# Side work kept in traced order, two more deferred key projections, later marks, a longer lead, and pair scans that carry their own first column

## The chip, the cores and the metric

The kernel runs on one core of one Trainium2 chip. The metric is the device time of one execution in microseconds (us), median over runs; lower is better.

## The reference

Two layers over a prompt of 2048 frames and a sample group of 64 frames (1024 features, 16 heads of 64). Layer 0 ("A") is attention in a band of chunks with a softmax; layer 1 ("B") is stick-breaking attention over all earlier frames, with a running product instead of a softmax. Both have a gate, an output projection and a residual.

```python
# layer 0, mixer A: per query chunk of 64, own chunk and 8 before it
q, k, v, gate = split(rms_norm(x, g) @ w_in_a)
x = x + (softmax(q @ k.T * SCALE + rel_bias, masked) @ v * silu(gate)) @ w_out_a
# shared keys and values, then layer 1, mixer B
k, v = split(rms_norm(x, g_kv) @ w_kv);  q, gate = split(rms_norm(x, g_b) @ w_in_b)
z = q @ k.T * SCALE;  log_fail = where(mask, log_sigmoid(-z), 0)
later = reverse_cumsum(log_fail) - log_fail
x = x + ((where(mask, exp(log_sigmoid(z) + later), 0) @ v) * silu(gate)) @ w_out_b
y = rms_norm(x)
```

Outputs are y for both groups and the new key and value rows of both layers.

## The kernel before

Every projection product is made from two parts of each operand (a rounded high part and the rest), so each block of 128 x 512 results takes 24 matmuls: 8 slices of the 1024 features, three products each. TensorE does these, the scores, the 128 x 128 turns ("flip") of attention weights, and the products with the values.

There are four stages in time. **A's projections** (`projections("a", ...)`): norms, values, then for each kind (k, q, gate) and each of the 8 head pairs `hp` two halves of 1024 frames. Where `(kind, hp)` is in `DEFER`, the second half is left out there and done later as side work. **A's attention** runs from about 753 us to 1335 us: head pair by head pair, 512-query groups in the order `ORDER = [(1, 0), (3, 2)]`. Then the rest of A's output projection; then **B's projections** and, from about 2078 us to 3260 us, **B's attention** in the same order (both with sample items beside), and the rest of B's output projection.

In an attention stage the class `Beat` writes the order of the code. One beat is one query tile: its scores, the turn and split of an older tile (`LAG`), the products of one older still (`HOLD`). `RATE` (0.4 a beat in A, 0.3 in B) lets in steps of side work from the list `beside`: late jobs (`late_job`: the deferred halves; 8 steps of 6 matmuls each, tile `ps_j`), the loading and splitting of the output weights (`w_out_steps`, tiles `woraw` to `big`), and output tiles (`out_tile`, tile `ps_o`, 8 steps of 6 matmuls each). Each unit of side work has `load` (DMAs issued on SP), `cut` (ACT rounds to the high part, DVE takes the rest) and the product steps. `load` of the next unit goes beside the first step of the present one, its `cut`s beside the second half. `lead(LEAD)` does the first steps before the first attention item. `when_summed` puts a group's output tiles on the list once its last head pair is done; they read back (`og`) what the attention stored (`o_a`, `o_b`).

The code's order is not the order of the engines' queues. A planner in the framework reorders the instructions of each engine's queue by its own cost estimates, under the data dependencies. `InOrder` can pin an instruction behind the one traced before it on its engine (`keep_in_program_order`), but its switch `order.on` is False everywhere in this kernel, so nothing is pinned.

In B, `pass_sticks` takes the running product over 512 keys, from the last to the first, two at a time: ACT makes `f`, POOL multiplies neighbours into `two` (256 columns), DVE scans `two` into every second column of `s`, and `between` on POOL first copies the carry (one column) into `s` and then fills the columns in between. Diagonal blocks scan all columns directly.

```python
            def between():
                to, carry = st
                gps.tensor_copy(to[:, CH : CH + 1], carry)
                gps.tensor_tensor(to[:, 1:CH:2], by2[:, :, 1], to[:, 2 : CH + 1 : 2], ALU.mult)
```

## Time and profile before

| what | value |
|---|---|
| time, median of 3 runs | 3362.42 us (3362.26 to 3369.03) |
| profiled execution, its own time | 3363.2 us |
| its span, first to last instruction | 3361.4 us |
| TensorE busy share, matmul / weight load | 96% / 83% |
| DVE, ACT, POOL busy share | 56%, 51%, 38% |

How to read it: PE is TensorE's matmuls, PEld its weight loads, DVE the vector engine, ACT the scalar engine, POOL GpSimd, SP the engine that issues most DMAs; a trailing q (SPq) is an engine's sequencer issuing or waiting. Each engine works its queue in order, so an instruction that waits holds all behind it. Almost all compute shows line L86, the helper that records every operation, so groups are told apart by the tiles that they write and read.

### The profile page before, as it was taken

What the parts mean: (1) busy time and instruction counts of PE and PEld (TensorE: products, weight loads), DVE (VectorE), ACT (ScalarE), POOL (GpSimd) and SP (SyncE); (2) the same over time, 40 slices, a digit from 0 to 9 for tenths busy, and PEclk for the clock granted to TensorE, in tenths of its full rate; (3) what the DMA queues carried; (4) which work ended last, traced back from release to release, by engine and by line L of the source; (5) the groups of instructions that cost most, each with busy time, mean ns of one, the idle gap of its engine ahead of it and who ended that gap; (6) DMA issues with size and microseconds to landing.
All of it is one profiled execution on the core that took longest, in us unless ns stands there. A gap on an engine that the chain in (4) does not pass through costs nothing.

```text
span 3361.4 us, 53483 instructions
## 1 busy us (share of the span) xinstructions
PE 3232.5 (96%) x17928; PEld 2801.8 (83%) x17928; DVE 1896.1 (56%) x3815; ACT 1723.1 (51%) x3716; POOL 1282.4 (38%) x1929
## 2 busy tenths in 40 slices
PE   8999999998999999999999999999999999999998
PEld 6889999986888888878889998778788787888777
DVE  3224431116886776322033333888888889888773
ACT  4323322226996776233144433666666676666661
POOL 2002210004774454021044200444476767777760
PEclk9999999998999999999999999999999999999999
DMA  5459984248998875544399857666735564445523
GB/s 188 140 176 362 338 318 155 95 146 258 253 241 221 240 215 151 188 138 137 106 338 352 294 184 226 178 186 189 192 103 140 155 181 127 129 128 152 139 89 110
DMA packets 454409, 643.30 MB, mean 191 GB/s; under 512 B 49733, under 2 KB 269925, under 8 KB 454134
## 3 DMA queue, kind: packets, MB, share of 16 engines
q1 hardware_dynamic: 394678, 588.75, 57.0%
q10 hardware_dynamic: 59456, 51.13, 4.7%
q8 instruction: 143, 2.34, 0.3%
q14 instruction: 132, 1.08, 0.1%
HBM read 388.85 MB, written 250.90 MB: 190 GB/s over the span
## 4 chain that ended last, share of the span: by engine, by line
PE 60%; DVE 7%; ACT 4%; DMA 3%; issue 3%; POOL 1%; SPq 0%; ACTq 0%; POOLq 0%; DVEq 0%
PE ps_o L86 10%; PE acc L86 10%; PE ps_t L86 10%; PE z L86 9%; PE wt L86 8%; PE ps_v L86 6%; PE ps_j L86 5%; DVE s L86 3%; DVE pl L86 2%; ACT ph L86 1%; ACT s L86 1%; DMA o_a<-ot 1%; ACT f L86 0%; DVE ol L86 0%; PE ps_tr L86 0%
## 5 line engine op out<-in xcount | busy, mean ns | idle before, releaser
L86 DVE TENSOR_TENSOR pl<-wt,ph 128x512 fp32r<-128x512 f32 (+1 forms) x864 | 551.8, 654 | 135.8 <-ACT ph L86 132.3
L86 ACT ACTIVATE ph<-wt 128x512 fp32r<-128x512 f32 (+1 forms) x864 | 483.7, 577 | 200.3 <-PE wt L86 183.4
L86 PE MATMUL wt<-ident,s 128*128 128x128 f32 x3472 | 552.6, 276 | 21.0 <-DVE pl L86 11.7
L86 PE MATMUL ps_t<-x_own,wh 128*128 128x362 f32 (+1 forms) x2304 | 569.9, 328 | 0.0
L86 PEld LDWEIGHTS wt<-ident,s 128*128 128x128 f32 x3472 | 418.5, 141 | 94.0 <-DVE pl L86 14.4
L86 ACT ACTIVATE f<-z 128x512 f32<-128x512 f32 (+4 forms) x680 | 355.3, 535 | 223.4 <-PE z L86 132.7
L86 POOL TENSOR_TENSOR s<-f,s 128x256 f32<-128x256 f32 x416 | 363.4, 874 | 122.0 <-DVE s L86 108.7
L86 PEld LDWEIGHTS ps_t<-x_own,wh 128*128 128x128 f32 x2304 | 404.8, 188 | 1.9
L86 PE MATMUL acc<-ph,vt 128*128 128x512 f32 (+3 forms) x1088 | 376.8, 381 | 20.5 <-ACT ph L86 14.3
L86 PE MATMUL acc<-pl,vt 128*128 128x512 f32 (+3 forms) x1088 | 368.3, 372 | 27.2 <-DVE pl L86 25.4
L86 PE MATMUL z<-kt,q 128*128 128x512 f32 (+3 forms) x1280 | 376.2, 381 | 11.3 <-ACT f L86 10.1
L86 PE MATMUL ps_t<-x_own,wl 128*128 128x362 f32 (+1 forms) x1152 | 377.4, 328 | 0.0
L86 POOL TENSOR_SCALAR s<-s,rc 128x640 f32<-128x640 f32 (+5 forms) x264 | 195.5, 748 | 469.6 <-DVE rc L86 419.0
L86 PE MATMUL ps_o<-big,oh 128*128 128x512 f32 x1088 | 338.8, 394 | 0.3 <-DVE pl L86 0.3
L86 POOL TENSOR_TENSOR two<-f 128x256 f32<-128x256 f32 x416 | 265.7, 641 | 168.4 <-ACT f L86 158.2
L86 DVE TENSOR_TENSOR_SCAN s<-two,s,own 128x256 f32<-128x256 f32 x408 | 299.6, 738 | 47.6 <-POOL two L86 41.9
L86 PE MATMUL ps_t<-big,wh 128*128 128x512 f32 x960 | 298.3, 391 | 0.0
L86 PEld LDWEIGHTS z<-kt,q 128*128 128x128 f32 x1280 | 220.3, 191 | 47.0 <-ACT f L86 23.8
L86 PEld LDWEIGHTS acc<-pl,vt 128*128 128x128 f32 x1088 | 196.2, 191 | 69.3 <-DVE pl L86 53.7
L86 PEld LDWEIGHTS acc<-ph,vt 128*128 128x128 f32 x1088 | 200.1, 192 | 46.6 <-ACT ph L86 21.0
L86 PEld LDWEIGHTS ps_o<-big,oh 128*128 128x128 f32 x1088 | 203.3, 189 | 42.0 <-DVE pl L86 0.9
L86 PEld LDWEIGHTS ps_t<-x_own,wl 128*128 128x128 f32 x1152 | 216.3, 188 | 0.1
(142 smaller groups left out, 5487.1 us busy)
## 6 DMA issues: line engine op xcount, KB each, us to landing
vt<-v_b SPq DMA_DIRECT2D x80, 512.0 KB, 5.1
v_b<-vs SPq DMA_DIRECT2D x64, 512.0 KB, 5.5
q<-q_a SPq DMA_DIRECT2D x128, 256.0 KB, 6.2
q<-q_b SPq DMA_DIRECT2D x128, 256.0 KB, 4.2
vt<-v_a SPq DMA_DIRECT2D x48, 512.0 KB, 8.1
kt<-k_b SPq DMA_DIRECT2D x96, 256.0 KB, 5.7
keys<-k_a SPq DMA_DIRECT2D x80, 256.0 KB, 6.7
v_a<-vs ACTq DMA_DIRECT2D x32, 512.0 KB, 2.7
```

The lines of the kernel that those rows point to most:

```text
L86: ins = op(*args, **kwargs)
```

## The change

1. `DEFER["a"]` holds the second half of the keys of head pairs 4 to 7 instead of 6 and 7: two more late jobs in A's attention.
2. `in_place` pins the `load` and `cut` steps of all side work to the traced order of SP, ACT and DVE while `order.amid` is set, that is from the end of `lead` to the end of the items. Products and what stands behind them are not pinned.
3. `SETTLE = 5`: output tiles come on the list five beats later.
4. `LEAD["b"]` is 14 instead of 8.
5. In the projections the sample's doubled columns live in a tile `x_new` of the pool tag `ol`, filled by two POOL copies, where `x_own[0]` had 64 more columns, filled by one ACT copy; the norm's `junk` gets a buffer of its own.
6. `two` becomes three persistent tiles of 257 columns whose last column is one. The scan runs over 257 columns and writes the carry itself (carry times one); the POOL copy in `between` goes.

```diff
--- before.py
+++ after.py
@@ -39,15 +39,17 @@
 
 SAMPLE = {(1, 0): [4, 3], (3, 2): [2, 1, 0]}
 
-DEFER = dict(a=[("k", 6), ("k", 7)], b=[(k, hp) for k in "gq" for hp in range(HP)])
+DEFER = dict(a=[("k", hp) for hp in (4, 5, 6, 7)], b=[(k, hp) for k in "gq" for hp in range(HP)])
 
 RATE = dict(a=0.4, b=0.3)
 LAG = dict(a=2, b=5)
 
-LEAD = dict(a=8, b=8)
+LEAD = dict(a=8, b=14)
 HOLD = dict(a=1, b=2)
 
 STEP = 2
+
+SETTLE = 5
 TOK = [(t * P, min(P, T - t * P)) for t in range((T + P - 1) // P)]
 
 HALF = NP // 2
@@ -73,7 +75,8 @@
 
 
     def __init__(self, tc):
-        self.tc, self.on = tc, False
+
+        self.tc, self.on, self.amid = tc, False, False
 
     def engine(self, engine):
         outer = self
@@ -99,6 +102,18 @@
     order = InOrder(tc)
     dve, act, gps, pe = (order.engine(x) for x in (nc.vector, nc.scalar, nc.gpsimd, nc.tensor))
     mm = pe.matmul
+
+    def in_place(what):
+
+
+        def pinned():
+            was, order.on = order.on, order.amid
+            what()
+            order.on = was
+
+        return pinned
+
+    sp = order.engine(nc.sync)
 
     cpool = ctx.enter_context(tc.tile_pool(name="consts", bufs=1))
     dram = ctx.enter_context(tc.tile_pool(name="scratch", bufs=1, space=DRAM))
@@ -194,17 +209,18 @@
             tc.tile_pool(name=f"pp_{L}", bufs=1, space=PSUM) as psum,
         ):
 
-
-            x_own = [xpool.tile([P, NK, HALF + m], F32R, name=f"x_own{i}") for i, m in enumerate((2 * NS, NS))]
+            x_own = [xpool.tile([P, NK, HALF + NS], F32R, name=f"x_own{i}") for i in range(2)]
             x_big = big_pair()
             xs = [x_own, x_big]
             with tc.tile_pool(name=f"v_{L}", bufs=2) as pool:
+
+                x_new = []
 
                 def normed(t, scale=gps.tensor_scalar):
                     r0, n = TOK[t]
                     xt = pool.tile([P, D], F32, name="xt", tag="xt", bufs=3)
                     nc.sync.dma_start(xt[:n], x_of(t))
-                    junk = opool.tile([P, D], mybir.dt.bfloat16, name="junk", tag="xr", bufs=2)
+                    junk = pool.tile([P, D], mybir.dt.bfloat16, name="junk", tag="junk", bufs=1)
                     r = rstd_of(pool, xt, n, junk)
                     scale(xt[:n], xt[:n], r[:n], 1.0, ALU.mult, ALU.mult)
                     ps = psum.tile([P, NK, P], F32, name="ps_tr", tag="tr", bufs=1)
@@ -213,7 +229,10 @@
                     hf, c = spot(r0)
                     split(*(x[:, :, c : c + n] for x in xs[hf]), ps[:, :, :n])
                     if n == NS:
-                        act.activation(x_own[0][:, :, NEW + NS :], f32(x_own[1][:, :, NEW:]), AF.Copy)
+
+                        x_new.append(opool.tile([P, NK, P], F32R, name="x_new", tag="ol", bufs=2))
+                        for i in range(2):
+                            gps.tensor_copy(x_new[0][:, :, i * NS : i * NS + NS], f32(x_own[i][:, :, NEW:]))
 
                 seq = [t for gs_ in ORDER for g in gs_ for t in range(4 * g, 4 * g + 4)] + [len(TOK) - 1]
                 if L == "a":
@@ -244,7 +263,7 @@
                         out = ps[:n]
                         if n == NS:
                             for k in range(NK):
-                                both = x_own[0][:, k, NEW:]
+                                both = x_new[0][:, k]
                                 mm(ps, both, wh[k], start=(k == 0), stop=False)
                                 mm(ps, both, wl[k], start=False, stop=(k == NK - 1))
                             out = pool.tile([P, CH], F32, name="vn", tag="vn", bufs=2)[:n]
@@ -638,7 +657,7 @@
         def load():
             st["raw"] = opool.tile([P, NK, P], F32, name="lraw", tag="og", bufs=1)
             c = c0 + hp * P
-            nc.sync.dma_start(st["raw"], w[:, c : c + P].rearrange("(k p) c -> p k c", p=P))
+            sp.dma_start(st["raw"], w[:, c : c + P].rearrange("(k p) c -> p k c", p=P))
             st["wh"] = opool.tile([P, NK, P], F32R, name="lwh", tag="oh", bufs=2)
             st["wl"] = opool.tile([P, NK, P], F32R, name="lwl", tag="ol", bufs=2)
 
@@ -694,7 +713,7 @@
             rows = kind == "k" and HALF + c >= first
             behind.append([partial(out, c)] + ([partial(add_back, c), (2, partial(token_rows, c))] if rows else []))
         products = [partial(some, c, k0) for c in chunks for k0 in range(0, NK, STEP)]
-        return [load] + [partial(cut, k0) for k0 in range(0, NK, STEP)], products, behind
+        return [in_place(x) for x in [load] + [partial(cut, k0) for k0 in range(0, NK, STEP)]], products, behind
 
     def w_out_steps(src, w):
 
@@ -704,7 +723,7 @@
             if k < NK:
                 tag = ("oh", "ol")[k % 2]
                 raws[k] = opool.tile([P, D], F32, name="woraw", tag=tag, bufs=2)
-                nc.sync.dma_start(raws[k], src[k * P : (k + 1) * P])
+                sp.dma_start(raws[k], src[k * P : (k + 1) * P])
 
         def cut(k):
             if k == 0:
@@ -715,7 +734,11 @@
             del raws[k]
 
         return [
-            ([partial(load, i) for i in range(3)] if k == 0 else [], [None], [[partial(cut, k), partial(load, k + 3)]])
+            (
+                [in_place(partial(load, i)) for i in range(3)] if k == 0 else [],
+                [None],
+                [[in_place(partial(cut, k)), in_place(partial(load, k + 3))]],
+            )
             for k in range(NK)
         ]
 
@@ -733,9 +756,9 @@
         def load():
             st["og"] = opool.tile([P, NK, P], F32, name="og", tag="og", bufs=1)
             src = lay[L]["o"][g][:, :, c0 : c0 + n].rearrange("k p t -> p k t")
-            nc.sync.dma_start(st["og"][:, :, :n], src)
+            sp.dma_start(st["og"][:, :, :n], src)
             st["xr"] = opool.tile([P, D], F32, name="xr", tag="xr", bufs=2)
-            nc.sync.dma_start(st["xr"][:n], residual(t))
+            sp.dma_start(st["xr"][:n], residual(t))
             st["oh"] = opool.tile([P, NK, P], F32R, name="oh", tag="oh", bufs=2)
             st["ol"] = opool.tile([P, NK, P], F32R, name="ol", tag="ol", bufs=2)
 
@@ -776,7 +799,7 @@
 
         products = [partial(some, c, k0) for c in range(0, D, CH) for k0 in range(0, NK, STEP)]
         cuts = [partial(cut, k0) for k0 in range(0, NK, NK // 2)]
-        return [load] + cuts, products, [[partial(out, 0)], [partial(out, CH), finish]]
+        return [in_place(x) for x in [load] + cuts], products, [[partial(out, 0)], [partial(out, CH), finish]]
 
     class Beat:
 
@@ -851,6 +874,7 @@
                 n -= 1
                 self.ready = 0
                 self.step()
+            order.amid = True
 
         def products(self):
             while self.held and self.held[0][0] + self.hold <= self.clock:
@@ -903,11 +927,12 @@
 
         def when_summed(self, what):
 
-            self.marks.append((self.blocks[-1][0] + 2 + self.hold, what))
+            self.marks.append((self.blocks[-1][0] + 2 + self.hold + SETTLE, what))
 
         def end(self):
             while self.tiles or self.blocks or self.held or self.marks:
                 self.beat()
+            order.amid = False
             while self.now or self.beside:
                 self.ready = 0
                 self.step()
@@ -1211,27 +1236,32 @@
                 return [lambda: None, scan]
 
             by2 = f.rearrange("p (j i) -> p j i", i=2)
-            two = pool.tile([P, CH // 2], F32, name="two", tag="two", bufs=2)
+            two = twos[0]
+            twos.append(twos.pop(0))
 
             def pairs():
-                gps.tensor_tensor(two, by2[:, :, 0], by2[:, :, 1], ALU.mult)
+                gps.tensor_tensor(two[:, :-1], by2[:, :, 0], by2[:, :, 1], ALU.mult)
 
             def scan():
                 to, carry = pr(), carry_in()
-                st.extend((to, carry))
+                st.append(to)
+
                 dve.tensor_tensor_scan(
-                    to[:, CH - 2 :: -2], two[:, ::-1], own[:, : CH // 2], carry, ALU.mult, ALU.bypass
+                    to[:, ::-2], two[:, ::-1], own[:, : CH // 2 + 1], carry, ALU.mult, ALU.bypass
                 )
                 passed(to[:, x0 : x0 + 1])
 
             def between():
-                to, carry = st
-                gps.tensor_copy(to[:, CH : CH + 1], carry)
+                to = st[0]
                 gps.tensor_tensor(to[:, 1:CH:2], by2[:, :, 1], to[:, 2 : CH + 1 : 2], ALU.mult)
 
             st = []
             return [pairs, scan, between]
 
+
+        twos = [wpool.tile([P, CH // 2 + 1], F32, name=f"two{i}") for i in range(3)]
+        for two in twos:
+            gps.memset(two[:, CH // 2 :], 1.0)
 
         totals = [wpool.tile([P, 2 * NS], F32, name=f"total{i}") for i in range(HP)]
         carries = [wpool.tile([P, 1], F32, name=f"carry{i}") for i in range(HP)]
```

## Rows read from the trace of the kernel before

**Rows 1.** The page, part 1: busy us (share of the span) xinstructions.

```profile
PE 3232.5 (96%) x17928; PEld 2801.8 (83%) x17928; DVE 1896.1 (56%) x3815; ACT 1723.1 (51%) x3716; POOL 1282.4 (38%) x1929
```

**Rows 2.** Windows: length, busy us of PE, PEld, DVE, ACT, POOL, clock, DMA.

```profile
220.00:753.00 533.00, 531.58 (x2867) 487.77 (x2866) 162.59 (x405) 155.42 (x392) 54.37 (x49) 1.00 0.68 237
753.00:860.00 107.00, 88.44 (x501) 76.49 (x502) 69.65 (x196) 73.69 (x172) 49.75 (x57) 0.92 0.89 263
860.00:1005.00 145.00, 134.13 (x913) 120.87 (x911) 120.41 (x371) 137.26 (x326) 106.16 (x129) 0.99 0.92 245
1005.00:1060.00 55.00, 48.52 (x295) 43.13 (x295) 36.07 (x90) 37.51 (x80) 23.84 (x26) 0.94 0.77 210
2080.00:2130.00 50.00, 41.92 (x212) 33.61 (x211) 34.22 (x57) 26.78 (x64) 16.46 (x29) 0.90 0.80 220
2760.00:2800.00 40.00, 31.42 (x151) 22.83 (x150) 38.91 (x56) 29.73 (x58) 25.38 (x38) 0.91 0.60 192
2800.00:3260.00 460.00, 448.05 (x2521) 367.02 (x2521) 388.47 (x613) 297.96 (x584) 338.11 (x614) 1.00 0.45 127
```

**Rows 3.** Timeline of TensorE, 755 to 770 us: start, duration, instruction.

```profile
759.63 0.62 PE L86 MATMUL ps_j<-big,lwh 128*128 128x512 f32 x2
...
762.80 0.39 PE L86 MATMUL ps_j<-big,lwl 128*128 128x512 f32 x1
```

**Rows 4.** Tile lraw: engine, operation, count, ns min/median/max.

```profile
L86 DVE SCALAR_TENSOR_TENSOR lwl<-lraw,g_b,lwh x128: 321/344/1369, 2054.5 to 2672.1; 128x128 fp32r<-128x128 f32 x128
L86 ACT ACTIVATE lwh<-lraw,g_a x16: 385/390/402, 727.9 to 754.1; 128x128 fp32r<-128x128 f32 x16
L86 DVE SCALAR_TENSOR_TENSOR lwl<-lraw,g_a,lwh x16: 350/352/353, 728.3 to 754.5; 128x128 fp32r<-128x128 f32 x16
```

**Rows 5.** Instructions on tile ps_j.

```profile
L86 ACT ACTIVATE sp<-ps_j x20: 575/597/605, 759.2 to 2760.5; 128x512 fp32r<-128x512 f32 x20
L86 DVE TENSOR_TENSOR sp<-ps_j,sp x20: 666/691/693, 759.8 to 2761.1; 128x512 fp32r<-128x512 f32 x20
```

**Rows 6.** Timeline, 1008 to 1015 us: start, duration, instruction, [idle before, releaser].

```profile
1008.10 0.37 SPq L736 DMA_DIRECT2D og<-o_a  x1
...
1012.22 1.15 ACT L86 ACTIVATE oh<-og 128x512 fp32r<-128x512 f32 x2 [6.24 <-DMA og<-o_a]
...
1013.91 0.80 PE L86 MATMUL acc<-ph,vt 128*128 128x256 f32 x2 [5.54 <-ACT ph L86]
```

**Rows 7.** Timeline, 2075 to 2092 us, the same columns.

```profile
2076.36 0.54 SPq L641 DMA_DIRECT2D lraw<-in_w_in_b  x1
...
2086.63 2.44 ACT L86 ACTIVATE lwh<-lraw,g_b 128x128 fp32r<-128x128 f32 x8 [4.51 <-DMA lraw<-in_w_in_b]
...
2089.61 2.08 PE L86 MATMUL z<-kt,q 128*128 128x512 f32 x4 [5.25 <-ACT f L86]
```

**Rows 8.** POOL groups by form, B's attention: busy us, mean ns, idle.

```profile
L86 POOL TENSOR_TENSOR two<-f 128x256 f32<-128x256 f32 x416 | 265.7, 641 | 168.4 <-ACT f L86 158.2 <-DVE lwl L86 7.8 <-DVE pl L86 0.9
L86 POOL COPY s<-s 128x1 f32<-128x1 f32 x408 | 79.6, 198 | 97.6 <-PE wt L86 41.9 <-DVE s L86 36.3 <-PE z L86 7.8
```

**Rows 9.** The same on DVE.

```profile
L86 DVE TENSOR_TENSOR_SCAN s<-two,s,own 128x256 f32<-128x256 f32 x408 | 299.6, 738 | 47.6 <-POOL two L86 41.9 <-PE wt L86 4.2
...
L86 DVE TENSOR_TENSOR big<-woraw,big 128x512 fp32r<-128x512 f32 x16 | 13.3, 856 | 0.0
```

**Rows 10.** Waits of TensorE, B's attention: us in total, times, longest.

```profile
PE acc L86 <- DVE pl L86: 24.3, 45, 2.7
```

**Rows 11.** Waits of DVE, the same stretch.

```profile
DVE s L86 <- POOL two L86: 42.6, 58, 3.8
```

**Rows 12.** Waits of SP's queue, the same stretch.

```profile
SPq L427 <- PE z L86: 169.6, 33, 23.0
```

**Rows 13.** Instructions on tile woraw, with its DMAs.

```profile
L707 SPq DMA_DIRECT2D woraw<-in_w_out_b x8: 332/336/497, 2713.7 to 2771.9; - x8
...
DMA to landing us min/median/max: 3.5/5.6/8.7
```

## Prediction

> **What bounds the kernel now.** I read the page's busy shares first, then windows by stage, then who waits for whom in each, then the timeline at the places where TensorE stops. TensorE is busy 3232.5 of 3361.4 us [rows 1], so 129 us of idle time is what the page offers; DVE, ACT and POOL are at half or less over the span. By stage it looks different [rows 2]. In A's projections (220 to 753 us) TensorE is busy 531.58 of 533 us at full clock and nothing else is near its limit: a matmul taken away there is time taken away. The start of A's attention (753 to 860 us) is the worst stretch: 18.6 us idle in 107, and a granted clock of 0.92, that is, (1 - 0.92) x 107 = 8.6 us lost to the lower of the two levels, 1.2 GHz, which it falls to after the stops. From 860 to 1005 us ACT is busy 137 of 145 us: there ACT is the limit. B's attention is near full on TensorE (448 of 460 us from 2800 us on), with DVE at 84% and POOL at 74% close behind, and two holes: its start (2080 to 2130 us, clock 0.90) and the stretch from 2760 to 2800 us, where DVE is busy 38.9 of 40 us.
>
> The Trainium skill (Perfetto Trace Analysis, Identifying the Most-Contended Engine) holds that matmul busy time is a poor measure of how near TensorE is to its limit, since matmuls overlap, and that the weight loads' busy share is better. The weight loads' row is at 83% [rows 1], which would leave 560 us and not 129; I keep the 129 us as the ceiling and give the larger room a rival below.
>
> **Two more deferred key pairs.** A late half is 2 blocks x 24 = 48 matmuls, two pairs 96. In a run of late-job matmuls 14 starts lie between 759.63 and 762.80 us [rows 3], 0.226 us each, so 96 x 0.226 = 21.7 us leave A's projections, where TensorE is the limit. They come back in A's attention, in the first beats after the lead of 8 steps, where TensorE has 18.6 + 8.6 = 27.2 us to give. Beside them come for ACT 2 x (8 weight roundings x 0.390 + 2 results x 0.597 + one copy of key rows, taken as another 0.6) = 9.8 us, and for DVE 2 x (8 x 0.352 + 2 x 0.691) = 8.4 us [rows 4, 5]; in 753 to 860 us ACT has 33 us and DVE 37 us idle, which hides it. If that cover is gone, because the jobs slip into the ACT-bound stretch, the 9.8 us show. Bounds: a gain of 27 if the holes and the low clock both go, nothing if every matmul lengthens the stage, a loss of 6 if ACT's two batches of 8 roundings (3.1 us each) also hold TensorE. I take -15, nearer to the full gain, because the stretch has holes on all engines.
>
> Against it: a DVE weight cut reads two operands, and while it took 0.350 to 0.353 us beside an idle POOL, its longest in B's attention was 1.369 us [rows 4]. The Trainium skill (SBUF — State Buffer, Who interferes with whom) says that a DVE instruction with two SBUF inputs contends with a GpSimd instruction that reads SBUF, and that the loser blocks for the other's whole instruction. If each of the 16 moved cuts were held so, 16 x (1.369 - 0.352) = 16.3 us of DVE would be added and this term would go from -15 to +1; by the median in B, 0.344 us, nothing is added. The median decides, but it feeds the flat rival.
>
> **Later marks and pinned cuts in A.** Where the first output tile's sums are read back, ACT stood 6.24 us on the rounding of `og`, whose load was issued at 1008.10 us, and TensorE then 5.54 us on an attention split behind it in ACT's queue [rows 6]. Five beats of settling, and a cut that stays in its traced place, put the load well ahead of its use. The stretch around it lost 5.5 us of wait and (1 - 0.94) x 55 = 3.3 us of clock [rows 2], so 8.8 at most, nothing if another load is late next. I take -6. At the stage's end the five beats push some 5 x 0.3 to 0.4 steps of 6 matmuls (2 to 3 us) out of the attention into the dense rest, where TensorE has work anyway: nothing.
>
> **B's start: pins and a longer lead.** ACT stood 4.51 us on a late job's weights, issued at 2076.36 us, did 8 roundings, and TensorE's next scores waited 5.25 us for ACT's `f` behind them [rows 7]. With 14 lead steps the first job, the end values and most of the second are done before the first item, and later cuts are pinned behind the items traced before. The hole costs 5.25 us and (1 - 0.90) x 50 = 5.0 us of clock [rows 2]; I take -6 of 10. The six more lead steps are 6 x 6 x 0.226 = 8.1 us of TensorE moved forward; as B's attention has TensorE as its limit they cost nothing net. If DVE's 84% turns out to be the real pace, they cost the 8.1 us.
>
> **The output weights in B.** From 2760 to 2800 us TensorE idles 8.6 us and loses (1 - 0.91) x 40 = 3.6 us of clock, because 16 DVE splits of `big` (13.3 us, [rows 9]) come in one go. Pinning changes where they stand, not how many: -3, between -12 and a loss that the slower rival prices.
>
> **The pair scans.** 408 one-column copies, 79.6 us of POOL, go [rows 8]; the scan grows by one column in 256, 738 / 256 x 408 = 1.2 us of DVE in all [rows 9]. POOL is not TensorE's direct releaser; the path is POOL's `two`, then DVE's scan (DVE waited 42.6 us for it, [rows 11]), then DVE's split `pl`, for which TensorE waited 24.3 us [rows 10]. Bounds: nothing, plus the 1.2 us, to -24. I take a quarter of the 24.3, -6. The three buffers of `two` in place of two only loosen a wait.
>
> **At nothing.** The sample's two POOL copies replace one ACT copy in each projection stage, on a POOL that is busy 54 of 533 us [rows 2]; by the nearest row (0.641 us for 256 columns [rows 8]) they are 2 x 1.3 us a stage, 5 us if all of it showed. The norm's own buffer has one writer and no reader.
>
> **Sum.** -15 - 6 - 6 - 3 - 6 = -36. The profiled execution took 3363.2 us, 1.8 more than its span and 0.8 more than the median, so 3327 for it and 3326 for the median.
>
> **Rivals.**
> *Flat.* The moved keys meet ACT (137 of 145 us just behind the holes), the copies were hidden, and only the two stalls at the read-back and B's start shrink by half: -7, 3355, between 3345 and 3368. For it: POOL hardly ever releases TensorE; the planner may place the unpinned products around the holes anew. Against: 18.6 us of idle time and 33 us of idle ACT stand at the very place where the keys go.
> *Slower.* Pinned loads stand in SP's queue behind every attention load traced before, and those wait for buffers: up to 23.0 us, for queries behind the scores [rows 12]. A weight row's load has three steps of 0.5 / 0.3 beats ahead of its cut, five beats of (3260 - 2078) / 680 = 1.74 us, 8.7 us; it landed in 5.6 us in the middle and 8.7 at most, and its first issue was at 2713.7 us, far ahead [rows 13]. A late load holds the pinned cut, and that holds ACT's `f` and `ph` and DVE's `pl`. Some 60 units of side work have such a load in the attention stages; at 1 us each that is +60 on the sum, 3387. It decides from 36 / 60 = 0.6 us a unit. Against: late jobs and output tiles have four steps, 13 beats or 23 us, of lead.
> *More.* All holes named go, with their clock: 27 + 8.8 + 10 + 12 + 24 = 82, 3281. For it speaks the weight loads' 83%; against, that five edits would each have to give all they can.
>
> **Chances.** Forecast 0.60 (own range 3305 to 3345), flat 0.20, slower 0.12, more 0.08. The range 3297 (four fifths of the 82) to 3368 (flat's upper end) leaves out more and slower. A difference under 0.2% (6.7 us) can't be told from none here: faster has the forecast, more and half of flat, 0.78; same the other half, 0.10; slower 0.12.
>
> **What would show it.** A's projections end some 22 us earlier and A's attention takes about 7 us more than before less the 6; the first 107 us of it at a clock nearer to 1 and with over 95 us of TensorE busy; no ACT wait on `og` above 2 us at the change of groups; no 4.5 us wait on `lraw` at B's start; POOL's busy time down by 80 us, DVE's wait for `two` well under 42 us. The prediction is wrong if A's attention grows by the full 22 us, or if ACT's waits on `woraw`, `og` or `lraw` grow to tens of us, or SP's waits ahead of L641, L707 and L736 do.

## The result and the profile after

The changed kernel took 3327.15 us (median of 4 runs, 3321.31 to 3329.61) against 3363.78 us for the kernel before (4 runs, 3362.26 to 3369.03): a ratio of 0.9886, 95% interval 0.9869 to 0.9903, or some 37 us less. The profiled execution took 3327.98 us with a span of 3326.2 us, 35.2 less than before.

The page's first part, after:

```profile
PE 3222.7 (97%) x17928; PEld 2800.3 (84%) x17928; DVE 1913.1 (58%) x3831; ACT 1723.2 (52%) x3730; POOL 1223.2 (37%) x1520
```

Beside [rows 1]: TensorE has the same 17928 matmuls and is busy 10 us less, POOL has 409 instructions less and is busy 59 us less, DVE has 16 and ACT 14 instructions more (16 extra weight cuts on each, and two ACT copies that went to POOL). The windows that answer to four of [rows 2], shifted to where the stages now lie (length, busy us of PE, PEld, DVE, ACT, POOL, granted clock, DMA):

```profile
220.00:727.00 507.00, 507.00 (x2752) 467.79 (x2752) 159.20 (x396) 149.63 (x380) 52.51 (x47) 1.00 0.69 243
729.00:836.00 107.00, 99.35 (x581) 86.47 (x582) 70.65 (x209) 75.78 (x183) 50.93 (x62) 0.97 0.86 250
2072.40:2122.40 50.00, 46.83 (x248) 38.92 (x247) 42.66 (x73) 30.16 (x69) 19.08 (x26) 0.93 0.72 200
2700.00:2745.00 45.00, 38.03 (x220) 29.73 (x218) 41.12 (x66) 31.47 (x65) 31.29 (x41) 1.00 0.84 242
```

The first 107 us of A's attention hold 581 matmuls for 501 before and TensorE is busy 99.35 us at a clock of 0.97, for 88.44 at 0.92. B's start, as far behind the first scores as in [rows 2] (third line), has 3.2 us idle for 8.1. The hole at the output weights is still there (fourth line, 7.0 us idle in 45). Its lower clock has gone in this execution; in run 9, whose engines have the same order of instructions in B, the same 45 us have a clock of 0.96, so the clock there differs between executions. To see where the 35 us come from, take the first and last start of some matmuls, from the instructions by tile. Before:

```profile
L86 PE MATMUL ps_t<-x_own,wl x1152: 322/327/420, 218.0 to 2065.6; 128*128 128x364 f32 x96, 128*128 128x362 f32 x96
```

```profile
L86 PE MATMUL z<-kt,q x1280: 219/392/796, 2077.7 to 3244.6; 128*128 128x512 f32 x123, 128*128 128x128 f32 x25, 128*128 128x384 f32 x25, 128*128 128x256 f32 x10
...
L86 PE MATMUL z<-keys,q x896: 221/309/689, 763.0 to 1328.1; 128*128 128x320 f32 x154, 128*128 128x256 f32 x7, 128*128 128x384 f32 x7, 128*128 128x128 f32 x6
```

```profile
L86 PE MATMUL ps_o<-big,oh x544: 387/389/628, 1014.5 to 1455.1; 128*128 128x512 f32 x182
```

After:

```profile
L89 PE MATMUL ps_t<-x_own,wl x1152: 322/327/420, 216.5 to 2048.7; 128*128 128x364 f32 x96, 128*128 128x362 f32 x96
```

```profile
L89 PE MATMUL z<-kt,q x1280: 218/393/775, 2070.1 to 3205.0; 128*128 128x512 f32 x123, 128*128 128x128 f32 x25, 128*128 128x384 f32 x25, 128*128 128x256 f32 x10
...
L89 PE MATMUL z<-keys,q x896: 221/309/668, 739.0 to 1305.0; 128*128 128x320 f32 x154, 128*128 128x256 f32 x7, 128*128 128x384 f32 x7, 128*128 128x128 f32 x6
```

```profile
L89 PE MATMUL ps_o<-big,oh x544: 387/389/794, 1011.4 to 1440.7; 128*128 128x512 f32 x182
```

Read as a chain of stretches, before and after: A's first scores 763.0 and 739.0 (-24.0); first to last scores 565.1 and 566.0 (+0.9); on to A's last output product 127.0 and 135.7 (+8.7); on to B's last projection 610.5 and 608.0 (-2.5); on to B's first scores 12.1 and 21.4 (+9.3, the longer lead); first to last scores of the prompt 1166.9 and 1134.9 (-32.0); on to the end 116.8 and 121.2 (+4.4). The sum is -35.2. By these starts 14.4 us had been won by A's last output product, and the rest behind it.

How far that split holds can be read from runs 6 and 11 below. They change B alone, and in layer A every engine works the same instructions in the same order as in the changed kernel. Their last output products of A:

```profile
L89 PE MATMUL ps_o<-big,oh x544: 387/389/795, 1013.0 to 1447.2; 128*128 128x512 f32 x182
```

```profile
L89 PE MATMUL ps_o<-big,oh x544: 387/389/501, 1010.1 to 1431.1; 128*128 128x512 f32 x182
```

1447.2 and 1431.1 us for 1440.7. First to last scores take 572.3 and 558.3 us for 566.0, and from there to the last output product it is 135.7 and 132.9 us for 135.7. Over the whole of it, 708.0, 691.2 and 701.7 us, the granted clock is 0.97, 0.99 and 0.98: the longer executions are those with the lower clock. So one execution tells where A ends to within some 16 us only. In the kernel before it differs less: 1454.5 to 1457.8 us over its own execution and those of runs 3, 4 and 8, with the same order in A.

The pair scans, in B's attention: waits of DVE and TensorE that answer to [rows 10, 11].

```profile
DVE s L89 <- POOL two L89: 15.4, 29, 1.3
```

```profile
PE acc L89 <- DVE pl L89: 18.9, 41, 2.0
```

DVE's wait for POOL fell by 27 us, TensorE's wait for DVE by only 5. POOL's busy time fell by 59 us and not by the copies' 79.6, because the records of its instructions overlap and the busy time counts overlapped time once: in the kernel before, a `two` that ends at 2901.38 us is followed by a copy that starts at 2901.32.

### The profile page after: what moved, and what is told of

Its sections match the earlier page's. It is cut to its first block, busy times and chain, and to the rows that moved or that the text cites. A ratio compares the mean times of both kernels' runs of the same rounds, so it can differ in the third digit from the quotient of the medians.

```text
span 3326.2 us, 53255 instructions
## 1 busy us (share of the span) xinstructions
PE 3222.7 (97%) x17928; PEld 2800.3 (84%) x17928; DVE 1913.1 (58%) x3831; ACT 1723.2 (52%) x3730; POOL 1223.2 (37%) x1520
## 4 chain that ended last, share of the span: by engine, by line
PE 80%; DVE 8%; DMA 5%; ACT 3%; issue 2%; POOL 1%; SPq 1%; ACTq 0%; POOLq 0%; DVEq 0%
PE ps_t L89 25%; PE ps_v L89 11%; PE ps_o L89 11%; PE acc L89 10%; PE z L89 8%; PE wt L89 8%; PE ps_j L89 5%; DVE s L89 3%; DVE pl L89 2%; ACT ph L89 1%; PE ps_tr L89 1%; DMA q<-q_a 1%; DMA vt<-v_b 1%; ACT s L89 1%; DVE lwl L89 1%
## 5 line engine op out<-in xcount | busy, mean ns | idle before, releaser
L89 DVE TENSOR_TENSOR pl<-wt,ph 128x512 fp32r<-128x512 f32 (+1 forms) x864 | 551.4, 653 | 119.8 <-ACT ph L89 116.8
L89 DVE TENSOR_TENSOR_SCAN s<-two,s,own 128x257 f32<-128x257 f32 x408 | 296.9, 737 | 19.8 <-POOL two L89 15.4
L89 PE MATMUL ps_t<-big,wh 128*128 128x512 f32 x896 | 278.6, 391 | 0.0
```

The source lines that it names most:

```text
L89: ins = op(*args, **kwargs)
```

## The experiments

In what follows a ratio is to the kernel before on the same chip and in the same job; the changed kernel's is 0.9886 (0.9869 to 0.9903). Each of runs 1 to 4 is the kernel before with one edit; runs 5 to 7 are the changed kernel without one; runs 8 to 12 change a size.

**1. Keys alone.**

```diff
-DEFER = dict(a=[("k", 6), ("k", 7)], ...)
+DEFER = dict(a=[("k", hp) for hp in (4, 5, 6, 7)], ...)
```

> The kernel before with the four deferred key pairs alone. My sum: A's projections end 22 us earlier, the moved products fall mostly into the holes at the start of A's attention, -15, so 3349. Rival (ACT is the limit there, or the side work is given back after the attention): A's attention or the output products behind it grow by as much as the projections lose, 3360 to 3364.

3350.87 us, ratio 0.9963 (0.9948 to 0.9979): about 12 us. The scores' first and last starts:

```profile
L89 PE MATMUL z<-keys,q x896: 222/309/686, 740.8 to 1316.4; 128*128 128x320 f32 x154, 128*128 128x256 f32 x7, 128*128 128x384 f32 x7, 128*128 128x128 f32 x6
```

The first scores come 22.2 us earlier (740.8 for 763.0), the last 11.7: A's attention took 575.6 us for 565.1. So half of the 21.7 us of products fell into holes and half lengthened the stage. The behaviour is the forecast's, the size (-12 for -15) near it. The halves are those of one execution.

**2. Pins alone.**

```diff
+            order.amid = True      # at the end of lead(); load and cut steps pinned from here
```

> The kernel before with the pinned loads and cuts alone (no settling, lead of 8). My sum: part of the 6 at A's read-back, of the 6 at B's start and the 3 at the output weights, about -8, so 3355. Rival (late loads hold ACT and DVE): waits on lraw, og or woraw of tens of us and a time above 3370. Second rival (order is the whole of the gain): -25 or more, 3338.

3349.26 us, ratio 0.9952 (0.9935 to 0.9969): about 16 us, twice what my terms gave to the pins. By the starts of its matmuls 3.5 us had been won by A's last output product and 14.2 at the end, most of it along B's attention.

**3. Pair scans alone.**

```diff
-                gps.tensor_copy(to[:, CH : CH + 1], carry)
-                    to[:, CH - 2 :: -2], two[:, ::-1], own[:, : CH // 2], carry, ALU.mult, ALU.bypass
+                    to[:, ::-2], two[:, ::-1], own[:, : CH // 2 + 1], carry, ALU.mult, ALU.bypass
...  (and the rest of item 6 of the change)
```

> The kernel before with the 257-column scans alone; 408 one-column copies on POOL go. My sum: -6, so 3357, DVE's wait for POOL's two falls from 42.6 us to half. Rival (POOL was hidden): within 3 us of before, whatever DVE's wait does. Second rival (POOL was worth more than a quarter of TensorE's waits on DVE): -12 or more.

3365.12 us over 10 runs, ratio 1.0001 (0.9989 to 1.0012): nothing. DVE's waits in B's attention:

```profile
DVE s L89 <- ACT f L89: 33.6, 20, 3.5
DVE s L89 <- POOL two L89: 24.5, 36, 2.3
```

The wait for `two` fell from 42.6 to 24.5 us, as expected, but the scans now waited for ACT's `f` longer, 33.6 us for 23.4 before: 10 of the 18 us came back. ACT's `f` in turn waits mostly for TensorE's scores (137.8 us). TensorE's wait for `pl` stayed (23.3 us for 24.3). POOL's own waits, over the whole kernel:

```profile
POOL two L89 <- ACT f L89: 303.1, 145, 23.9
...
POOL s L89 <- DVE s L89: 85.7, 98, 3.1
```

It waits 303.1 us for `f`, where [rows 8] has 158.2, and 85.7 for DVE's scan, where the kernel before has 145.0: together 85.6 us more, about the 80 of the copies. Their time has become waiting for `f`. The planner also put B's queues in another order than in the kernel before (the first TensorE matmul that differs is the 113th from B's first late job on), so the run measures the edit together with that order.

**4. Lead alone.**

```diff
-LEAD = dict(a=8, b=8)
+LEAD = dict(a=8, b=14)
```

> The kernel before with the lead of 14 steps in B alone. My sum: most of the stall at B's start goes and the 8.1 us of products moved forward come off later, -4, so 3359. Rival (the attention's pace is not TensorE's, so what is moved forward is not given back): +4 to +8, 3367 to 3371.

3358.66 us over 10 runs, ratio 0.998 (0.997 to 0.9991): about 7 us for the 4 forecast. But the stall at B's start did not go with it, as run 7 shows next to this one.

**5. The changed kernel without settling.**

```diff
-SETTLE = 5
+SETTLE = 0
```

> The changed kernel without settling (marks five beats earlier), all else as changed. My term for the read-back was 6 with the pins: about 5 slower than the changed kernel, 3332, with ACT waiting on og at the change of groups. Rival (settling only moves output products from the attention to the dense rest, so it gives and takes back): A's attention longer by some 15 us, the rest behind it shorter by 10, and the time within 3 us of the changed kernel.

3332.72 us, ratio 0.9907 (0.989 to 0.9925): some 5 to 7 us slower than with it, but the intervals overlap, so neither the forecast nor the rival is decided by the time. The place forecast is there, at the change of groups (timeline: start, duration, instruction, idle before):

```profile
998.18 0.38 SPq L89 DMA_DIRECT2D og<-o_a  x1
...
1004.03 1.15 ACT L89 ACTIVATE oh<-og 128x512 fp32r<-128x512 f32 x2 [3.73 <-DMA og<-o_a]
...
1004.71 1.22 PE L89 MATMUL ps_o<-big,oh 128*128 128x512 f32 x2 [3.44 <-ACT oh L89]
```

ACT stands 3.73 us on the load of `og` and TensorE 3.44 us for ACT. With settling, the same place in the changed kernel:

```profile
1010.69 1.16 ACT L89 ACTIVATE oh<-og 128x512 fp32r<-128x512 f32 x2
...
1011.38 0.73 PE L89 MATMUL ps_o<-big,oh 128*128 128x512 f32 x2 [0.52 <-ACT oh L89]
```

The first products wait 0.52 us. Whether A ends earlier for it is not shown. The pattern is the rival's: the last scores start at 1305.0 with settling and 1314.4 without, while A's last output product starts at 1440.7 with and 1440.8 without; but with settling it lies between 1431.1 and 1447.2 over three executions. The products pushed behind the attention are only part of it, as the windows from A's last scores to its last output product show, without settling and with it:

```profile
1314.40:1440.80 126.40, 125.91 (x600) 105.25 (x599) 45.44 (x82) 37.78 (x75) 14.51 (x17) 1.00 0.48 155
```

```profile
1305.00:1441.00 136.00, 133.19 (x617) 110.83 (x616) 45.36 (x80) 37.20 (x74) 15.75 (x17) 0.97 0.44 144
```

17 matmuls more, about 3.6 us by the mean of 0.21 us; but TensorE also idles 2.8 us for 0.5, and in this execution the clock of 0.97 costs 0.03 x 136 = 4.1 us. The stops are behind the attention's last item, at the output tiles that settling pushed there:

```profile
1330.06 0.28 ACT L89 ACTIVATE total<-acc 128x128 f32<-128x128 f32 x1 [5.21 <-PE acc L89]
...
1332.82 2.07 PE L89 MATMUL ps_o<-big,oh 128*128 128x512 f32 x4 [2.51 <-ACT oh L89]
...
1338.62 1.15 ACT L89 ACTIVATE oh<-og 128x512 fp32r<-128x512 f32 x2 [5.33 <-DMA og<-o_a]
```

ACT stands 5.21 us for the end of the attention's sums, its rounding of the next tile waits in the queue behind that, TensorE stands 2.51 us for the rounding, and the tile after it waits 5.33 us for its load. The low clock does not come with these stops each time. The 30 us from 5 us behind the last scores on, in the changed kernel and in run 11, with the same 2.8 us idle:

```profile
1310.00:1340.00 30.00, 27.19 (x143) 23.02 (x143) 11.61 (x22) 13.18 (x26) 6.90 (x7) 0.89 0.27 96
```

```profile
1303.20:1333.20 30.00, 27.19 (x156) 23.30 (x155) 11.53 (x22) 13.20 (x26) 6.94 (x7) 1.00 0.28 96
```

So a stall came up at the stage's end, and what lies behind the last scores takes 132.9 to 135.7 us in three executions with settling, for 126.4 without and 127.0 in the kernel before. The profiled spans are 4.7 us apart, which is less than A's end differs between executions of one order.

**6. The changed kernel with the old pair scans.** The edit of run 3 the other way round.

> The changed kernel with the old pair scans (256 columns, a one-column copy on POOL, two buffers). If POOL is hidden, as the scans alone said, the time stays within 3 us of the changed kernel, 3327. Rival (POOL shows once pins and lead have made B's attention denser): 5 to 10 slower, 3332 to 3337, with DVE's wait for two back at 40 us.

3329.07 us, ratio 0.9892 (0.9865 to 0.9919): not to be told from the changed kernel; but the interval is 9 us to either side and holds the 6 us forecast too, so it is run 3 that speaks against them. The rival's sign, a wait for `two` of 40 us, did not come:

```profile
DVE s L89 <- POOL two L89: 29.2, 52, 1.5
DVE s L89 <- ACT f L89: 20.2, 15, 3.1
```

With the new scans these are 15.4 and 19.4 us: here the wait for `f` did not rise. TensorE's wait for `pl` is 15.7 us with the old scans and 18.9 with the new ones.

**7. The changed kernel with nothing pinned.**

```diff
-            order.amid = True
+            order.amid = False
```

> The changed kernel with nothing pinned, all else as changed. If the pins are worth the same beside the other edits as alone: 15 slower, 3342, most of it in B's attention, with a stall again where the output weights are split. Rival (settling and the lead already keep loads ahead of use): 3 to 6 slower, 3331.

3343.15 us, ratio 0.9934 (0.9918 to 0.9951): 16 us slower, as much as the pins gave alone. B's start, without and with pins:

```profile
2063.69 2.45 ACT L89 ACTIVATE lwh<-lraw,g_b 128x128 fp32r<-128x128 f32 x8 [5.07 <-DMA lraw<-in_w_in_b]
...
2078.20 0.38 SPq L89 DMA_DIRECT2D lraw<-in_w_in_b  x1
...
2083.34 0.69 ACT L89 ACTIVATE lwh<-lraw,g_b 128x128 fp32r<-128x128 f32 x2 [2.37 <-DMA lraw<-in_w_in_b]
```

```profile
2076.91 0.68 ACT L89 ACTIVATE lwh<-lraw,g_b 128x128 fp32r<-128x128 f32 x2
...
2083.81 0.69 ACT L89 ACTIVATE lwh<-lraw,g_b 128x128 fp32r<-128x128 f32 x2
```

Without pins the planner puts a job's roundings into ACT's queue ahead of weights that have not landed: ACT stands 5.07 us, then 2.37 us. In the changed kernel they come two at a time and ACT does not wait for them. The pins alone do not do that: in run 2, with its shorter lead, all 8 roundings still stand in one go and wait longer:

```profile
2094.80 2.45 ACT L89 ACTIVATE lwh<-lraw,g_b 128x128 fp32r<-128x128 f32 x8 [6.58 <-DMA lraw<-in_w_in_b]
```

The first 100 us after B's first scores, by windows, for the kernel before, the pins alone, the lead alone, the changed kernel without pins, and the changed kernel:

```profile
2077.70:2177.70 100.00, 88.36 (x484) 72.16 (x483) 76.91 (x135) 59.71 (x138) 35.83 (x63) 0.95 0.73 203
```

```profile
2073.80:2173.80 100.00, 87.26 (x491) 71.53 (x490) 80.63 (x139) 62.27 (x142) 38.22 (x67) 0.97 0.76 201
```

```profile
2088.20:2188.20 100.00, 89.22 (x490) 74.44 (x489) 77.99 (x135) 59.97 (x134) 37.62 (x67) 0.93 0.71 197
```

```profile
2069.50:2169.50 100.00, 89.51 (x488) 73.86 (x487) 77.12 (x134) 60.07 (x134) 34.84 (x47) 0.93 0.69 191
```

```profile
2070.10:2170.10 100.00, 95.90 (x542) 80.72 (x541) 84.99 (x147) 64.31 (x149) 41.58 (x54) 0.97 0.71 201
```

484, 491, 490 and 488 matmuls, and 542 with both. Neither the pins nor the lead closes the hole; together they bring the busy time from 88.4 to 95.9 us. Run 6 has both and the old scans, and 545 matmuls, so the new scans are not needed for it. The stall forecast at the output weights did not come back: between the last late job's product and the first output product TensorE idles 8.2 us without pins and 7.7 with them; the clock there is 0.86 for 1.00, each in one execution.

**8. Copies twice, in the kernel before.**

```diff
                 gps.tensor_copy(to[:, CH : CH + 1], carry)
+                gps.tensor_copy(to[:, CH : CH + 1], carry)
```

> The kernel before with every one-column carry copy on POOL done twice, some 80 us more of POOL in B's attention. If POOL has that room (74 to 75% busy), within 3 us of before. Rival (POOL stands on the path): 6 to 12 slower, 3370 to 3376, with DVE's wait for two above 60 us and TensorE's wait on DVE's pl above 30.

3377.8 us over 10 runs, ratio 1.0047 (1.0034 to 1.0059): 16 us slower. So the edit that takes 80 us from POOL gives nothing and the one that adds 80 costs 16. DVE's waits:

```profile
DVE s L86 <- POOL two L86: 48.6, 57, 3.1
DVE s L86 <- ACT f L86: 44.2, 24, 3.7
```

The rows fit the rival's size but not its path: the wait for `two` went only to 48.6 us, below the 60 expected; the wait for `f` nearly doubled, 23.4 to 44.2.

**9. Six pairs deferred, in the changed kernel.**

```diff
-DEFER = dict(a=[("k", hp) for hp in (4, 5, 6, 7)], ...)
+DEFER = dict(a=[("k", hp) for hp in (2, 3, 4, 5, 6, 7)], ...)
```

> The changed kernel with the second half of the keys of six head pairs deferred (2 to 7) instead of four. A's projections end another 22 us earlier. If A's attention has TensorE holes left to fill, some 10 us more gain, 3317. Rival (the holes are used up by the first two pairs, the next ones lengthen the attention by their full matmul time and ACT's roundings): attention 22 to 30 us longer, 3327 to 3335.

3335.3 us, ratio 0.9931 (0.991 to 0.9952): 15 us slower than with four.

```profile
L89 PE MATMUL z<-keys,q x896: 220/309/660, 715.7 to 1310.2; 128*128 128x320 f32 x154, 128*128 128x256 f32 x7, 128*128 128x384 f32 x7, 128*128 128x128 f32 x6
```

The first scores come 23.3 us earlier than with four pairs, the attention takes 594.5 us for 566.0. The third pair of jobs gives back 28.5 us, more than it took away: the rival.

**10. The output weights at half the pace.**

```diff
-            return 1.0 if product else 0.5
+            return 1.0
```

> The changed kernel with one step of the output weights costing a whole side step instead of half, so their loads and splits are spread over twice the beats. If the hole at the output weights comes from DVE and ACT being flooded with splits: 4 to 8 faster, 3320. Rival (the hole is TensorE without side products, whatever the pace of the splits): same to 6 slower, 3327 to 3333.

3322.03 us, ratio 0.9886 (0.987 to 0.9902): the changed kernel's ratio again, as the rival has it. But in B the splits were spread less than meant: from the first to the last it is 43.1 us (2713.2 to 2756.3) for 32.5, and DVE is busy 19.1 of 20 us in the hole:

```profile
2720.00:2740.00 20.00, 15.81 (x86) 12.14 (x84) 19.08 (x31) 16.14 (x33) 12.02 (x17) 0.91 0.80 263
```

So the run does not settle whether a flooded DVE makes the hole. For the rival speaks that the hole lies each time between the last late job's product and the first output product, where TensorE has no side products: 2760 to 2808 us before, 2702 to 2748 after, 2690 to 2759 here. The cause stays open.

**11. A lead of 20.**

```diff
-LEAD = dict(a=8, b=14)
+LEAD = dict(a=8, b=20)
```

> The changed kernel with a lead of 20 steps in B's attention instead of 14. Six more steps are 8.1 us of products ahead of the attention. If what the lead bought was the stall at B's start, that is gone already and the time is within 3 us of 3327; if moved products come off in full and more later, another 4 faster; rival (side work runs out before the last group's sums are there): 4 to 8 slower.

3327.84 us, ratio 0.9908 (0.9887 to 0.9928), an interval that overlaps the changed kernel's: not settled, and no gain shown. The profiled execution is 4.8 us shorter, but its layer A, with the same order, ended 9.6 us earlier. At B's start a hole is back, with 476 matmuls for 542:

```profile
2058.80:2158.80 100.00, 89.41 (x476) 73.66 (x475) 70.59 (x122) 52.33 (x120) 30.81 (x42) 0.95 0.70 198
```

**12. Cuts twice for A's late jobs, in the changed kernel.**

```diff
+            for _ in range(2 if L == "a" else 1):
                 scaled_split(st["wh"][:, ks], st["wl"][:, ks], st["raw"][:, ks], g[:, ks])
```

> The changed kernel with the weight cuts of A's four late jobs done twice: 32 roundings on ACT (12.5 us) and 32 splits on DVE (11 us) more, some of them ahead of the attention, the products unchanged. If ACT sets the pace where the moved keys run, so that the roundings are what they give back: 8 to 12 slower than the changed kernel, 3336 to 3339. If TensorE's own time is what they give back: within 4, 3324 to 3331.

3324.8 us, ratio 0.9882 (0.9864 to 0.99). The counts show that the work was there:

```profile
L89 ACT ACTIVATE lwh<-lraw,g_a x64: 384/396/407, 704.0 to 840.8; 128x128 fp32r<-128x128 f32 x64
L89 DVE SCALAR_TENSOR_TENSOR lwl<-lraw,g_a,lwh x64: 323/351/1440, 704.5 to 841.4; 128x128 fp32r<-128x128 f32 x64
```

64 roundings and 64 splits, and no loss that shows; the difference to the changed kernel is known to some 8 us either way. Of the 32 more on each engine 18 start behind the first scores, 7.0 us of ACT at 0.39. They are felt at the place, for the first 107 us hold 560 matmuls for 581:

```profile
729.00:836.00 107.00, 96.02 (x560) 82.86 (x561) 76.20 (x222) 78.69 (x196) 48.87 (x59) 0.97 0.86 252
```

The attention as a whole is as long as before, 565.6 us for 566.0. So ACT's and DVE's cuts are the less likely price of the moved keys, by the time, but a part of it is not excluded. The Trainium skill (SBUF — State Buffer, Who interferes with whom) says that a DVE instruction with two SBUF inputs contends with a GpSimd instruction that reads SBUF. The trace agrees as far as it goes: 8 of the 64 splits took over 0.5 us, up to 1440 ns, each of them with a POOL instruction beside it, while the median is 351 ns.

No run beats the changed kernel by more than its interval.

## Why the prediction was right, and where a step was not

The time (3326 forecast, 3327.15 measured), the sign and the likeliest case held. That the sum came so near is partly luck: the pair scans missed by 6 us one way, and the pins by some 8 the other.

**Two more key pairs: -15 forecast, -12 measured (run 1).** The 21.7 us leave the projections in full (A's first scores 22.2 us earlier), and about half comes back as longer attention; the forecast had a third coming back. That A's attention is 0.9 us longer in the changed kernel, where the prediction's signs have 7 less 6, is luck in its closeness: the executions of runs 6 and 11 have it 7.2 longer and 6.8 shorter. Which engine decides was the open point between this term and the flat rival. Run 12 speaks against ACT: 12.5 us more of roundings, 7.0 of them in the attention, show no loss in the time. That it is TensorE's own time was not measured and is not shown. Run 9 gives the limit: once the holes are used, two more pairs cost more than they free.

**Read-back in A: -6 forecast; the stall is gone, a gain is not shown (run 5).** The mechanism at the place was right. The step that failed is that the five beats at the stage's end cost "nothing" since "TensorE has work anyway": the products themselves are 3.6 us, about the 2 to 3 reckoned, but the tiles now behind the last item bring their own waits for ACT and `og`, and A's rest grew by 5.9 to 8.7 us against the kernel before (132.9 to 135.7 us for 127.0). Of a stall moved elsewhere the prediction asked what is late next in the middle, not at the end. The 5 to 7 us by which the kernel is slower without settling are within the intervals.

**Pins and lead at B's start: -6 forecast.** Here the price was low and the reasoning incomplete: the hole needs both edits (484 matmuls in the first 100 us before, about 490 with either, 542 with both, and 476 again with a lead of 20). All pins together are worth 16 us, alone as well as within the change (runs 2, 7), against some 8 in the forecast. B's start accounts for part of it. In run 2 the other part is spread over B's attention without one stall that carries it, and what makes it up was not separated.

**The output weights: -3.** The hole stayed in B and moved with the end of the late jobs. That the 16 DVE splits make it was argued and is not shown: run 10 left DVE as full there, and the time the same.

**The pair scans: -6 forecast, nothing measured (runs 3, 6).** This is the failed step: "a quarter of the 24.3" us for which TensorE waited on DVE. DVE's wait for POOL did fall, from 42.6 us to 24.5 and 15.4, and TensorE's wait for DVE did not follow: 23.3 us for 24.3 in run 3, and 18.9 with the new scans for 15.7 with the old ones in the changed kernel. In run 3 part of DVE's wait came back as a wait for ACT's `f`, and POOL itself waited for `f` in the time of its copies. By the time the flat rival's clause, that the copies were hidden, was the right one; the interval of run 3 leaves 4 us either way. What else the new order of the queues gave or took was not separated.

**The slower rival** did not come: ACT no longer waits on `lraw` at all, and the longest of SP's waits on `z` that answer to [rows 12] is 17.3 us for 23.0. But its kind of loss is there in small: ACT's waits on `og` are 23.8 us in all for 10.7, none above 2 us at the change of groups, as forecast, and the long ones (5.33, 7.08, 4.88 and 4.51 us) behind the last items of A and B. **More** did not come either: against the 560 us that the weight loads' share would leave, all six edits and the sizes tried gave 37. Where TensorE is busy all of 507 us (220 to 727 us, above), the weight loads' row shows 92%, so 83% is not 17% of room.

Adding up the four edits measured alone: 12 + 16 + 0 + 7 = 35 us, by their ratios, and 5 to 7 that are not clear of noise for settling; the change as a whole gave 37. Within the intervals the edits add. The sample's columns and the norm's buffer were not tried alone.

## What to carry to other kernels

A list of waits tells how long an engine stood, not what its next limit is: before pricing a shorter producer by the waits on it, look at what the consumer would wait for instead. Work moved from a stage where TensorE is full into one with holes pays until the holes are full and then costs its whole time (28.5 us for 23.3 in run 9), so size it by the holes' length. Where a planner orders the queues, pinning the steps that wait for a DMA was worth 16 us here; with too short a lead a pinned step still stood 6.58 us. And before a stretch of one execution is compared with that of another, it pays to look at how far two executions of the same order differ there.

## What was unexpected of the hardware

The first of three observations is on the granted clock: with the same order of instructions and the same 2.8 us of idle time, the 30 us behind A's last scores were granted a clock of 0.89, a mean over its two levels, in the changed kernel and 1.00 in run 11 (lines in run 5). The second goes with it: layer A of one order ended 16 us later in one execution than in another, at a mean clock of 0.97 for 0.99. What decides the clock in such a case is not shown.

The third is that the room on POOL looks one-sided. By the windows from 2900 to 3100 us (2910 to 3110 in run 8), POOL is busy 132.87 us in run 3, 145.50 in the kernel before and 158.25 in run 8, of 200; the time is the same in the first two and 16 us longer in the third. The windows hold 85 instructions fewer and 85 more than the kernel before, so a copy is worth 12.6 / 85 = 0.15 us. A tile of pairs takes POOL 0.641 us for `two` [rows 8] and 0.874 for the products into `s` (its group on the page of before), 1.51 us; with one copy 1.66, with two 1.81 by this estimate. The windows hold 85 such tiles in 200 us, one in 2.35 us, so POOL does not run out of time on the mean, and a threshold is not shown. From the first to the last scores of the prompt TensorE idles 61.9 us in run 8 for 50.6 in the kernel before; the order of its queue also differs in places in both run 3 and run 8, and the load on POOL and the order were not separated.

```profile
2900.00:3100.00 200.00, 195.53 (x1103) 162.03 (x1102) 169.26 (x265) 128.16 (x250) 145.50 (x264) 1.00 0.49 135
```

```profile
2910.00:3110.00 200.00, 195.81 (x1100) 161.37 (x1099) 165.82 (x265) 127.65 (x251) 158.25 (x349) 1.00 0.48 136
```

```profile
2900.00:3100.00 200.00, 194.47 (x1098) 161.95 (x1098) 165.29 (x263) 126.04 (x248) 132.87 (x179) 1.00 0.47 132
```
